# h's operands without the norm's factor, pair products in block 0, and another order of VectorE's work on a pair and on the bank sums

## The chip, the cores and the metric

The kernel runs on one core of one Trainium2 chip. The metric is the device time of one execution in microseconds (us); the kernel before takes 1032.63 us, the median of three runs (1032.61 to 1032.65). Five engines work side by side, each through its own list of instructions in order: TensorE (PE, matmuls and transposes), VectorE (DVE), ScalarE (ACT), GpSimd (POOL) and SyncE (SP, which issues most loads). They wait for each other by semaphores.

## The reference

One layer on 256 rows of 2048 values: a mix of differential attention and a convolution, projected and added to x, and then a SwiGLU block. The change is in the second half:

```python
h = h + jnp.einsum('bsm,md->bsd', mixed, w_out[l])
hn = rms_norm(h, norm2_g[l])
a = jnp.einsum('bsd,df->bsf', hn, w_gate[l])
bu = jnp.einsum('bsd,df->bsf', hn, w_up[l])
h = h + jnp.einsum('bsf,fd->bsd', jax.nn.silu(a) * bu, w_down[l])
```

rms_norm multiplies each row of h by one factor, 1 / sqrt(mean of its squares + eps), and each column by a gain. All is fp32; the hidden width is 5632.

## The kernel before

**Products.** An fp32 matrix is split in a high part (rounded by a cast on ScalarE) and a low part (what is left, a subtraction on VectorE), and each product is three matmuls: high by high, low by high, high by low. The rows are two tiles of 128 (m = 0, 1), the columns are taken in blocks of 512. A *chunk* is two 128-row slices of a weight: a load of 128x1024 (`raw`), a cast to `whi`, a subtraction to `wlo`, and 12 matmuls of 128x512. A *pair* ("s" in the tables) takes two slices of the gate weight and two of the up weight (`wb`, 128x2048) together and makes of them seven products instead of eight: ScalarE casts three of the tiles to high parts (L1052), VectorE makes four sums and differences of them (`wt`, L1049 to L1051), ScalarE casts these (L1055), VectorE makes the low parts `wlb` (L1058) and `wlt` (L1059), and TensorE does 21 matmuls (L1076 to L1078) into several PSUM banks q. The activations' side of a pair is a set of seven sums and differences of h's quarters, the *forms* (`fhi`, `flo`), made once by `make_forms`.

**The stages that matter.** The out-projection computes h in four column blocks n = 0 to 3; n = 3 comes last, in eight chunks. `out_done(n)` adds each block to h (L828), sums squares for the norm, has TensorE transpose the new columns (`ps_h`, L846, two times four transposes a block), scales them by the gain, and splits them in `hhi` and `hlo`. The feed-forward part follows in 11 blocks of 512 hidden columns, in groups of 4, 4 and 3, each group with a pass through w_down. Block 0 is plain: 8 chunks of gate and 8 of up with h's 16 slices; the norm's factor `rstd2` of each row comes in behind, with the silu (`silu_done`, `up_done`). While block 0 runs, `make_forms` spreads the factor over a tile by two transposes (`ps_r`, L988), multiplies the transposed h by it (`hn`, L996), and makes from that the operands of all later blocks: `chi` and `clo` for the slices that go through chunks, and the forms. Blocks from 1 on are 4 pairs and 8 chunks ("g" of gate, "u" of up) in an order written as a string. Behind the last gate chunk or pair, `bank_sums` adds the banks up on VectorE, `products_done` takes the silu, and behind the block `block_done` adds the rest, multiplies, and has the result transposed (`ps_a`).

**What sets the order.** The program is written chunk by chunk: `run_chunks` loads and casts a chunk up to three ahead (near a pair; else two), splits it two ahead, then issues its matmuls. All else (the out-projection's ends, the forms, the sums) are generators; each takes one step when a chunk's matmuls are half issued and one when all are (`resume`), a pair takes four. A `lag(n)` is n such steps. The engines keep to the order so written. Tiles come from pools: `pre` holds what stages before the feed-forward part need and is closed when h's last columns are transposed; only then `ffn` opens over the same memory. Some low parts (`BY_DMA`) are made by an accumulating DMA of GpSimd instead of VectorE.

Of the kernel before, what the change touches and what calls it, by code (L numbers as in the profile page):

```python
# [12 lines left out]
F32 = mybir.dt.float32  # L13
# [5 lines left out]
P = 128  # L19
# [14 lines left out]
LINE = 128  # L34
EPS = 1e-6
# [51 lines left out]
FIRST_ORDER = "gsggsgsuusuu"  # L87
# [42 lines left out]
def tile_block(  # L130
# [13 lines left out]
    prestack = ExitStack()  # L144
    pre = prestack.enter_context(tc.tile_pool(name="pre", bufs=2))
    small = prestack.enter_context(tc.tile_pool(name="small", bufs=4))
# [4 lines left out]
    h = [pre.tile([P, D], F32, tag=f"h{m}", name=f"h{m}", bufs=1) for m in range(NM)]  # L151
# [325 lines left out]
    def square_sum(src, accum, **kw):  # L477
        junk = pre.tile([P, N], F32, tag="junk", name="junk", bufs=1)
        act.activation(junk[:, : src.shape[-1]], src, AF.Square, accum_out=accum, **kw)
# [106 lines left out]
    def conv_back(b):  # L586
# [37 lines left out]
        for b in range(2):  # L624
            for t in range(NB // 2):
# [6 lines left out]
                for j in range(2):  # L632
# [3 lines left out]
                    hi = pre.tile([P, S], F32R, tag="mchi", name=f"mchi{ct}", bufs=NCT)  # L636
                    lo = pre.tile([P, S], F32R, tag="mclo", name=f"mclo{ct}", bufs=NCT)
# [135 lines left out]
    def attend_values(hd):  # L773
# [29 lines left out]
        for e in range(2):  # L803
            mixa[2 * hd + e] = lhs_pair("a", 2 * hd + e) if hd >= 2 else tuple(
                pre.tile([P, S], F32R, tag=t, name=t, bufs=4) for t in ("mahi", "malo"))
            act.activation(mixa[2 * hd + e][0], pt[:, e, :], AF.Copy, scale=col("sg", e))
# [6 lines left out]
    hT = {}  # L813

    hn = []
# [9 lines left out]
    def out_done(n, ps):  # L825
        cs = slice(n * N, (n + 1) * N)
# [13 lines left out]
        for t in range(0, N // P, 2):  # L840
# [6 lines left out]
            if k % HK == 0:  # L847
                hn.append(early.tile([P, HK, S], F32, tag="wb", name="hn"))
            rows = hn[k // HK][:, k % HK : k % HK + 2, :]
            for i in range(2):  # L850
                act.activation(rows[:, i, :], pt[:, i, :], AF.Copy, scale=col("g2", k + i))
# [3 lines left out]
            for i in range(2):  # L855
                hT[k + i] = (hi[:, i, :], lo[:, i, :])
# [3 lines left out]
        else:  # L860
            yield
            yield
            prestack.close()
            ffn["pool"] = ctx.enter_context(tc.tile_pool(name="ffn", bufs=1))
            start(make_forms())


    ffn = {}
    actT = {}
    sil = {}  # L870

    def silu_done(ps):
        yield
        for m in range(NM):
            sil[m] = ffn["pool"].tile([P, N], F32, tag=f"sum{m}", name="sil")
            act.activation(sil[m], ps[m], AF.Silu, scale=rstd2[m])

    def up_done(j, ps):
        fp = ffn["pool"]
        aa = []  # L880
        for m in range(NM):
            a = fp.tile([P, N], F32, tag=f"sum{2 + m}", name="a")
            dve.scalar_tensor_tensor(a, ps[m], rstd2[m], sil[m], ALU.mult, ALU.mult)
            aa.append(a)
        yield from lag(4)
        yield from transposed(j, aa)

    def transposed(j, aa):
        last = j + 1 in FIRSTS and NDS[group_of(j)[0]] < HD
        b = j - group_of(j)[1]  # L890
        for t in range(N // P // 2):
# [9 lines left out]
            if b < 2 and 2 * t < nd:  # L901
                if not b and not t:
                    raw_act[g] = ffn["pool"].tile([P, 2, nd, S], F32, tag="draw", name="raw_act")
# [30 lines left out]
    def make_down_forms(g):  # L934
# [20 lines left out]
        hs = ffn["pool"].tile([P, 2, nd, P], F32R, tag="dhs", name="dhs")  # L955
# [12 lines left out]
        ls = ffn["pool"].tile([P, 4, nd, P], F32R, tag="draw", name="dls")  # L968
# [407 lines left out]
```

## Time and profile before

The profiled execution's own time is its span of 1030.8 us, 1.8 us under the median of the runs, which takes in what lies around the span.

| | |
|---|---|
| median of 3 runs | 1032.63 us |
| span of the profiled execution | 1030.8 us |
| TensorE clock granted | 1.000 |
| DMA, mean over the span | 232 GB/s |
| casts of weights on ScalarE (L326), 256 of them | 264.2 us |
| wlo on VectorE (L335), 208 of them | 250.4 us |
| wlt on VectorE (L1059), 61 of them | 139.8 us, and 19.7 us of waiting for the cast L1055 |

In the profile a row of a timeline is: start, length, engine, line, operation, output<-inputs, sizes and type, how many in a row; in brackets the time for which the engine stood idle before it and what it waited for. The length of a matmul's row is from its entry to its end; since matmuls are pipelined, the distance between starts is what one costs. The same holds for VectorE and ScalarE in a small measure.

### The profile page before, as it was taken

What the parts mean: (1) busy time and instruction counts of PE and PEld (TensorE: products, weight loads), DVE (VectorE), ACT (ScalarE), POOL (GpSimd) and SP (SyncE); (2) the same over time, 40 slices, a digit from 0 to 9 for tenths busy, and PEclk for the clock granted to TensorE, in tenths of its full rate; (3) what the DMA queues carried; (4) which work ended last, traced back from release to release, by engine and by line L of the source; (5) the groups of instructions that cost most, each with busy time, mean ns of one, the idle gap of its engine ahead of it and who ended that gap; (6) DMA issues with size and microseconds to landing.
All of it is one profiled execution on the core that took longest, in us unless ns stands there. A gap on an engine that the chain in (4) does not pass through costs nothing.

```text
span 1030.8 us, 13034 instructions
## 1 busy us (share of the span) xinstructions
PE 1025.7 (100%) x4642; PEld 849.4 (82%) x4642; DVE 929.2 (90%) x1128; ACT 643.4 (62%) x786; POOL 102.7 (10%) x146
## 2 busy tenths in 40 slices
PE   9999999999999999999999999999999999999998
PEld 8888888888888888888888888888888888888887
DVE  6899999999765699999999898989999989889998
ACT  7644656665756675676666556667757556657562
POOL 0300112111000000100102101101001111010020
PEclk9999999999999999999999999999999999999999
DMA  9757555544466677997989799889798979897776
GB/s 338 254 194 258 190 184 164 158 169 166 141 215 214 197 262 222 282 265 210 254 259 272 251 257 270 258 234 262 228 269 255 285 207 283 247 267 218 226 200 174
DMA packets 116448, 238.64 MB, mean 232 GB/s; under 512 B 7840, under 2 KB 9120, under 8 KB 116384
## 3 DMA queue, kind: packets, MB, share of 16 engines
q1 hardware_dynamic: 105216, 203.58, 59.3%
q0 software_dynamic: 10880, 34.08, 17.0%
q8 instruction: 36, 0.59, 0.2%
q14 instruction: 28, 0.23, 0.1%
q10 hardware_dynamic: 288, 0.16, 0.1%
HBM read 204.24 MB, written 9.44 MB: 207 GB/s over the span
## 4 chain that ended last, share of the span: by engine, by line
PE 100%; POOL 0%; DVE 0%; issue 0%; POOLq 0%
PE acc L365 11%; PE acc L366 11%; PE acc L371 11%; PE q L1097 11%; PE q L1103 11%; PE q L1098 11%; PE q L1078 9%; PE q L1077 9%; PE q L1076 9%; PE ps_a L898 1%; PE ps_s L712 1%; PE ps_o L782 1%; PE ps_warm L164 0%; PE ps_h L846 0%; PE ps_qk L693 0%; PE ps_at L802 0%
## 5 line engine op out<-in xcount | busy, mean ns | idle before, releaser
L326 ACT CAST whi<-raw 128x1024 fp32r<-128x1024 f32 (+1 forms) x256 | 264.2, 1043 | 143.8 <-PE acc L366 86.6
L335 DVE TENSOR_TENSOR wlo<-raw,whi 128x1024 fp32r<-128x1024 f32 (+1 forms) x208 | 250.4, 1214 | 38.2 <-ACT whi L326 38.0
L1055 ACT CAST wh<-wt 128x2048 fp32r<-128x2048 f32 x61 | 116.8, 1915 | 109.9 <-DVE wt L1051 109.7
L1059 DVE TENSOR_TENSOR wlt<-wt,wh 128x2048 fp32r<-128x2048 f32 x61 | 139.8, 2291 | 19.8 <-ACT wh L1055 19.7
L1097 PE MATMUL q<-whi,chi 128*128 128x512 f32 x320 | 125.2, 391 | 0.0
L1098 PE MATMUL q<-whi,clo 128*128 128x512 f32 x320 | 124.6, 389 | 0.0
L365 PE MATMUL acc<-whi,xhi 128*128 128x512 f32 x312 | 124.1, 398 | 0.0
L366 PE MATMUL acc<-whi,xlo 128*128 128x512 f32 x312 | 122.2, 392 | 0.0
L1076 PE MATMUL q<-wh,fhi 128*128 128x512 f32 x280 | 109.8, 392 | 0.0
L1077 PE MATMUL q<-wh,flo 128*128 128x512 f32 x280 | 109.0, 389 | 0.0
L1058 DVE TENSOR_TENSOR wlb<-wb,wh 128x1536 fp32r<-128x1536 f32 x61 | 106.8, 1751 | 1.0 <-ACT wh L1052 1.0
L572 DVE SCALAR_TENSOR_TENSOR y<-upad,cw,y 128x256 f32<-128x256 f32 x240 | 101.6, 490 | 0.0
L330 POOL DMA_DIRECT2D wlo<-raw x48 | 41.5, 865 | 555.7 <-ACT wlo L329 286.3
L1052 ACT CAST wh<-wb 128x1536 fp32r<-128x1536 f32 x61 | 89.8, 1472 | 1.0 <-DMA wb<-in_w_down_dram 1.0
L1103 PE MATMUL q<-wlo,chi 128*128 128x512 f32 x320 | 85.7, 390 | 0.0
L371 PE MATMUL acc<-wlo,xhi 128*128 128x512 f32 x312 | 85.2, 394 | 0.0
L1049 DVE TENSOR_TENSOR wt<-wb 128x1024 f32<-128x1024 f32 x61 | 74.4, 1220 | 0.0
L1097 PE MATMUL q<-whi,ahi 128*128 128x512 f32 x182 | 71.0, 390 | 0.0
L1098 PE MATMUL q<-whi,alo 128*128 128x512 f32 x182 | 70.9, 389 | 0.0
L1103 PEld LDWEIGHTS q<-wlo,chi 128*128 128x128 f32 x320 | 60.0, 188 | 12.7 <-DMA wlo<-raw 0.3
L1097 PEld LDWEIGHTS q<-whi,chi 128*128 128x128 f32 x320 | 60.1, 188 | 12.3
L1098 PEld LDWEIGHTS q<-whi,clo 128*128 128x128 f32 x320 | 60.1, 188 | 12.2
(260 smaller groups left out, 1850.5 us busy)
## 6 DMA issues: line engine op xcount, KB each, us to landing
raw<-in_w_in_dram SPq DMA_DIRECT2D x78, 512.0 KB, 4.6
raw<-in_w_gate_dram SPq DMA_DIRECT2D x48, 512.0 KB, 5.0
raw<-in_w_up_dram SPq DMA_DIRECT2D x48, 512.0 KB, 5.3
wlo<-raw POOLq DMA_DIRECT2D x48, 512.0 KB, 7.1
raw<-in_w_down_dram SPq DMA_DIRECT2D x46, 512.0 KB, 6.2
wb<-in_w_down_dram SPq DMA_DIRECT2D x42, 512.0 KB, 5.9
wb<-in_w_up_dram SPq DMA_DIRECT2D x40, 512.0 KB, 4.4
wb<-in_w_gate_dram SPq DMA_DIRECT2D x40, 512.0 KB, 5.5
```

The lines of the kernel that those rows point to most:

```text
L326: act.copy(c["hi"], c["raw"])
L335: dve.tensor_tensor(c["lo"], c["raw"], c["hi"].bitcast(F32), ALU.subtract)
L365: pe.matmul(ps[m], xhi[:, ms], hi[:, j, :], start=c["first"] and j == 0, stop=False)
L366: pe.matmul(ps[m], xlo[:, ms], hi[:, j, :], start=False, stop=False)
L371: pe.matmul(ps[m], xhi[:, ms], lo[:, j, :], start=False, stop=c["last"] and j == nk - 1)
L1055: act.copy(c["hi"][:, :SUMMED], c["t"])
L1059: dve.tensor_tensor(lot, c["t"], c["hi"][:, :SUMMED].bitcast(F32), ALU.subtract)
L1076: pe.matmul(ps, hi, c["hi"][:, w], start=bool(first), stop=False)
L1077: pe.matmul(ps, lo, c["hi"][:, w], start=False, stop=False)
L1097: pe.matmul(ps, xs[i][0][:, ms], hi[:, i, :], start=i == 0 and bool(c["first"].get(qs[m])), stop=False)
L1098: pe.matmul(ps, xs[i][1][:, ms], hi[:, i, :], start=False, stop=False)
L1103: pe.matmul(sum_bank(c, qs[m]), xs[i][0][:, ms], lo[:, i, :], start=False, stop=i == 1 and bool(c["last"].get(qs[m])))
```

## The change

- **Factor.** h's operands carry the gain only. The norm's factor comes in at the silu of each block: `products_done` gives it to the Silu as its scale, and multiplies the silu by it once more with a Copy on ScalarE (so silu(a) times the factor, which makes up for the up half). `rep`, `ps_r`, `rb`, the four multiplications of `hn`, the `hhi`/`hlo` splits of h and the plain block's `silu_done` and `up_done` go.
- **Operands.** `out_done` writes `chi` and `clo` from the transposes in PSUM (n = 1 and 3) or the rows that the forms are made of (n = 0 and 2). The forms are started behind n = 2, so that they are made while n = 3 is multiplied.
- **Block 0** becomes a block of 4 pairs and 8 chunks, in the order "gugsgsgsusuu"; it takes its banks from the two PSUM pools the other way round (`swap`), and none of its low parts by DMA.
- **Pools.** What lives to the end of the out-projection (h, the small tiles, the operands of the mix) moves to `keep` and `small`; `ffn` opens at n = 0, and a pool `late` (wlb, wlt, the sums) opens when h's last columns are transposed, on the memory of `keep`. A pair's first low part therefore waits for the last copies of h to memory.
- **A pair on VectorE.** The four sums, the low parts and now two casts of 1024 are written in turn instead of one kind after the other.
- **Bank sums.** The six additions come in another order.

```diff
-FIRST_ORDER = "gsggsgsuusuu"
+ORDERS = {0: "gugsgsgsusuu", 1: "gsggsgsuusuu"}
...
     def out_done(n, ps):
+        if not n:
+            prestack.close()
+            ffn["pool"] = fp = ctx.enter_context(tc.tile_pool(name="ffn", bufs=1))
...
-            hi, lo = lhs_two("h", k)
-            act.copy(hi, rows)
-            dve.tensor_tensor(lo, rows, hi.bitcast(F32), ALU.subtract)
+            if k % HK < NS:
+                rows = ffn["rows"][:, k // HK, k % HK : k % HK + 2, :]
+                for i in range(2):
+                    act.activation(rows[:, i, :], pt[:, i, :], AF.Copy, scale=col("g2", k + i))
+            else:
+                a = REST.index(k)
+                hi, lo = (ffn[x][:, a : a + 2, :] for x in ("chi", "clo"))
+                for i in range(2):
+                    act.activation(hi[:, i, :], pt[:, i, :], AF.Copy, scale=col("g2", k + i))
+                for i in range(2):
+                    dve.scalar_tensor_tensor(lo[:, i, :], pt[:, i, :], col("g2", k + i), hi[:, i, :].bitcast(F32),
+                                             ALU.mult, ALU.subtract)
...
+        if n == HK * P // N:
+            yield
             start(make_forms())
+        if n == D // N - 1:
+            yield
+            yield
+            keepstack.close()
+            ffn["late"] = ctx.enter_context(tc.tile_pool(name="late", bufs=1, side="right"))
...
     def round_pair(c):
-        assert "pair" in forms
+        while "pair" not in forms or "late" not in ffn:
+            resume()
...
     def split_pair(c):
-        act.copy(c["hi"][:, :SUMMED], c["t"])
-        dve.tensor_tensor(lob, c["b"][:, 1:], c["hi"][:, SUMMED:].bitcast(F32), ALU.subtract)
-        dve.tensor_tensor(lot, c["t"], c["hi"][:, :SUMMED].bitcast(F32), ALU.subtract)
+        act.copy(hi[:, 2:SUMMED], t[:, 2:])
+        rest(lob[:, :1], b[:, 1:2], hi[:, SUMMED : SUMMED + 1])
+        next(sums, None)
+        rest(lob[:, 1:], b[:, 2:], hi[:, SUMMED + 1 :])
+        next(sums, None)
+        act.copy(hi[:, :2], t[:, :2])
+        rest(lot[:, 2:], t[:, 2:], hi[:, 2:SUMMED])
+        rest(lot[:, :2], t[:, :2], hi[:, :2])
...
         dve.tensor_tensor(u2, q[Q6], w1, ALU.add)
+        dve.tensor_tensor(w1, q[Q2], w1, ALU.add)
         dve.tensor_tensor(u3, q[Q7], u2, ALU.add)
+        dve.tensor_tensor(u2, q[Q5], u2, ALU.add)
         dve.tensor_tensor(w4, q[Q5], u3, ALU.add)
-        dve.tensor_tensor(u2, q[Q5], u2, ALU.add)
-        dve.tensor_tensor(w1, q[Q2], w1, ALU.add)
         dve.tensor_tensor(u3, q[Q4], u3, ALU.add)
...
-        for t in g:
-            act.activation(t, t, AF.Silu)
+        for m, t in enumerate(g):
+            act.activation(t, t, AF.Silu, scale=rstd2[m])
+            act.activation(t, t, AF.Copy, scale=rstd2[m])
```

`rest(lo, raw, h)` is the subtraction of a low part; `next(sums, None)` writes the next of the two sums t[1] and t[0], whose lines were L1050 and L1051; t[2:4] (L1049) is now written by `first_sums` from `round_pair`.

The first place is TensorE's list where the out-projection ends and block 0 begins. Before (mchi is the mix's operand, hhi h's, acc the banks; the last out chunk's end, the first gate chunk, the first transposes of h's last columns):

```order
L371 MATMUL acc<-wlo,mchi_2868 128x512
L365 MATMUL acc<-whi,hhi_2958 128x512
L366 MATMUL acc<-whi,hlo_2959 128x512
...
L371 MATMUL acc<-wlo,hhi_2958 128x512 x4
L846 MATMUL ps_h<-ident,h_81 128x128
L846 MATMUL ps_h<-ident,h_82 128x128
L846 MATMUL ps_h<-ident,h_81 128x128
L846 MATMUL ps_h<-ident,h_82 128x128
L365 MATMUL acc<-whi,hhi_2983 128x512
```

And now:

```order
L374 MATMUL acc<-wlo,mchi_2875 128x512
L852 MATMUL ps_h<-ident,h_88 128x128
L852 MATMUL ps_h<-ident,h_89 128x128
L852 MATMUL ps_h<-ident,h_88 128x128
L852 MATMUL ps_h<-ident,h_89 128x128
L852 MATMUL ps_h<-ident,h_88 128x128
L852 MATMUL ps_h<-ident,h_89 128x128
L852 MATMUL ps_h<-ident,h_88 128x128
L852 MATMUL ps_h<-ident,h_89 128x128
L1085 MATMUL q_3371<-whi,chi 128x512
```

All eight transposes of n = 3 now stand directly behind the out-projection's last matmul and ahead of the first gate chunk (since `round_pair` of the first pair, three chunks ahead, takes steps of the generators until `late` is open); before, the first four stood behind that chunk and the other four in the middle of the next.

The second place is VectorE's list at the same point, from the additions of n = 2 to the first pair. Before (the forms then stand in block 0, further down):

```order
L828 TENSOR_TENSOR h_82<-h_82,acc 128x512
L854 TENSOR_TENSOR hlo_3166<-hn,hhi_3165 128x512
L335 TENSOR_TENSOR wlo<-raw,whi 128x1024
L854 TENSOR_TENSOR hlo_3191<-hn,hhi_3190 128x512
L335 TENSOR_TENSOR wlo<-raw,whi 128x1024 x7
L828 TENSOR_TENSOR h_81<-h_81,acc 128x512
L828 TENSOR_TENSOR h_82<-h_82,acc 128x512
```

And now, from the forms' third operation on:

```order
L989 TENSOR_TENSOR sums<-hn 128x512
L990 TENSOR_TENSOR sums<-hn,sums 128x512
L995 TENSOR_TENSOR flo<-hn,fhi 128x512 x2
L338 TENSOR_TENSOR wlo<-raw,whi 128x1024
L997 SCALAR_TENSOR_TENSOR flo<-hn,fhi 128x512
L998 TENSOR_TENSOR flo<-sums,fhi 128x512
L1000 TENSOR_TENSOR flo<-sums,fhi 128x1536
L338 TENSOR_TENSOR wlo<-raw,whi 128x1024 x3
L834 TENSOR_TENSOR h_88<-h_88,acc 128x512
L834 TENSOR_TENSOR h_89<-h_89,acc 128x512
L842 TENSOR_REDUCE ssh<-ss_0_143 128x1
L842 TENSOR_REDUCE ssh<-ss_1_144 128x1
```

The forms moved from block 0 to between the low parts of the out-projection's last chunks; one low part fewer stands ahead of h's additions.

The third place is VectorE's list for a pair. Before, the second pair of block 1:

```order
L1049 TENSOR_TENSOR wt<-wb 128x1024
L1050 TENSOR_TENSOR wt<-wb,wt 128x512
L1051 TENSOR_TENSOR wt<-wt,wb 128x512
L1058 TENSOR_TENSOR wlb<-wb,wh 128x1536
L1059 TENSOR_TENSOR wlt<-wt,wh 128x2048
L335 TENSOR_TENSOR wlo<-raw,whi 128x1024
```

And now, the first pair of block 0:

```order
L1024 TENSOR_TENSOR wt<-wb 128x1024
L338 TENSOR_TENSOR wlo<-raw,whi 128x1024
L1038 TENSOR_TENSOR wlb<-wb,wh 128x512
L1028 TENSOR_TENSOR wt<-wb,wt 128x512
L1038 TENSOR_TENSOR wlb<-wb,wh 128x1024
L1029 TENSOR_TENSOR wt<-wt,wb 128x512
L1038 TENSOR_TENSOR wlt<-wt,wh 128x1024 x2
```

No operation reads what the one directly ahead of it wrote; there are seven for a pair where there were five.

More of the change, by code (lines that the diff above doesn't have):

```diff
@@ L825, in out_done @@
     def out_done(n, ps):
+        if not n:
+            prestack.close()
+            ffn["pool"] = fp = ctx.enter_context(tc.tile_pool(name="ffn", bufs=1))
+            ffn["rows"] = fp.tile([P, 2, NS, S], F32, tag="wh", name="hn", bufs=2)
+            for t in ("chi", "clo"):
+                ffn[t] = fp.tile([P, len(REST), S], F32R, tag=t, name=t)
         cs = slice(n * N, (n + 1) * N)
@@ L859, in out_done @@
             h_squares(n, cs)
-        else:
+        if n == HK * P // N:
+            yield
+            start(make_forms())
+        if n == D // N - 1:
             yield
             yield
-            prestack.close()
-            ffn["pool"] = ctx.enter_context(tc.tile_pool(name="ffn", bufs=1))
-            start(make_forms())
+            keepstack.close()
+            ffn["late"] = ctx.enter_context(tc.tile_pool(name="late", bufs=1, side="right"))
     ffn = {}
+    plain = {}
     actT = {}
[L870 to L886, printed above, removed]
     def transposed(j, aa):
@@ L1131, in multiply_two, with fast_block @@
             start(c["done"](c["sums"]))
-    def fast_block(order, pairs, twos, sources, operands, half, whole, by_dma=dict(g=(), u=())):
+    def fast_block(order, pairs, twos, sources, operands, half, whole, by_dma=dict(g=(), u=()), swap=False):
         units, sums = [], {}
@@ L1138, in fast_block @@
             what = left[kind].pop(0)
-            c = dict(kind=kind, sums=sums, done=None, first={}, last={}, rows=what["rows"], **operands)
+            c = dict(kind=kind, sums=sums, swap=swap, done=None, first={}, last={}, rows=what["rows"], **operands)
             if kind == "s":
@@ L1158, in gate_up_block @@
     def gate_up_block(j):
[L1159 removed]
+        fast_block(ORDERS.get(j, ORDER), [dict(p=p, rows=slice(p, p + HK + 1, HK)) for p in range(NS)],
                    [dict(ks=ks, rows=slice(ks[0], ks[1] + 1, ks[1] - ks[0]), k=ks) for ks in TWOS],
                    dict(g=(w_gate, j * N), u=(w_up, j * N)),
[L1162 removed]
+                   dict(pairs=lambda: forms.get("pair"), plain=plain.get),
                    products_done, lambda sums: block_done(j, sums),
[L1164 removed]
+                   BY_DMA if j > 1 and j not in FIRSTS else dict(g=(), u=BY_DMA["u"] if j else ()), swap=not j)
     def down_pass(g, j0, nb):
@@ L1183, in bank_sums @@
     def bank_sums(q):
-        w1, u2, u3, w4 = (ffn["pool"].tile([P, N], F32, tag=f"sum{i}", name=f"sum{i}") for i in range(4))
+        w1, u2, u3, w4 = (ffn["late"].tile([P, N], F32, tag=f"sum{i}", name=f"sum{i}") for i in range(4))
         act.copy(w1, q[Q1])
@@ L1306, in tile_block @@
         for j in range(j0, j0 + nb):
[L1307 to L1313 removed]
+            gate_up_block(j)
         down_pass(g, j0, nb)
```

102 lines of the change are left out of this document (36 added, 66 removed).

## The prediction

> **What bounds the kernel now.** The page comes first: who is busy, at what clock, and through whom the chain that ended last runs.
>
> ```profile
> PE 1025.7 (100%) x4642; PEld 849.4 (82%) x4642; DVE 929.2 (90%) x1128; ACT 643.4 (62%) x786; POOL 102.7 (10%) x146
> PEclk9999999999999999999999999999999999999999
> PE 100%; POOL 0%; DVE 0%; issue 0%; POOLq 0%
> ```
>
> TensorE is busy for 1025.7 of 1030.8 us, at full clock in every slice, and the whole chain is its own work. So time is won only by fewer matmuls, and lost wherever TensorE is made to wait. VectorE comes next with 90%. The windows show where its slack lies: the out-projection's last columns, block 0, block 1.
>
> ```profile
> 280.00:338.00 58.00, 58.00 (x271) 47.68 (x270) 35.72 (x45) 34.98 (x56) 3.48 (x6) 1.00 0.59 200
> 338.00:383.00 45.00, 45.00 (x205) 37.13 (x204) 37.36 (x40) 29.85 (x40) 1.99 (x4) 1.00 0.69 221
> 383.00:424.00 41.00, 41.00 (x187) 33.95 (x186) 39.19 (x35) 27.27 (x25) 2.79 (x4) 1.00 0.85 259
> ```
>
> After the length, the busy times are PE, weight load, DVE, ACT, POOL. DVE (third) has 7.6 us free in block 0 and only 1.8 us in block 1. The change makes block 0 a block like block 1, behind a place where DVE has much to do. So TensorE's and DVE's timelines there are what counts.
>
> ```profile
> 338.31 0.39 PE L365 MATMUL acc<-whi,hhi 128*128 128x512 f32 x1
> ...
> 341.03 0.67 PE L846 MATMUL ps_h<-ident,h 128*128 128x128 f32 x4
> 341.46 0.48 PE L365 MATMUL acc<-whi,hhi 128*128 128x512 f32 x1
> ...
> 343.40 0.60 PE L846 MATMUL ps_h<-ident,h 128*128 128x128 f32 x4
> 343.75 1.17 PE L371 MATMUL acc<-wlo,hhi 128*128 128x512 f32 x4
> ...
> 350.22 0.38 PE L988 MATMUL ps_r<-ident,rep 128*128 128x128 f32 x2
> ...
> 383.10 0.39 PE L1097 MATMUL q<-whi,chi 128*128 128x512 f32 x1
> ...
> 386.28 0.39 PE L1078 MATMUL q<-wlt,fhi 128*128 128x512 f32 x1
> ```
>
> Block 0 starts at 338.31, block 1 at 383.10; at 386.28 the first pair of block 1 takes its low parts (wlt, the last thing DVE makes for a pair). From 338.31 to 341.03 are 12 matmuls: 0.227 us each, 2.72 a chunk, 4.76 a pair (21). Four transposes take 0.43 and 0.35, so about 0.11 each. Behind 386.28 the two programs issue the same matmuls, and TensorE doesn't wait there now; **when this matmul can start after the change, plus any later new wait, is the answer.**
>
> **The change part by part.** *TensorE alone.* Block 0 falls from 16 chunks (192 matmuls) to 4 pairs and 8 chunks (180): 12 x 0.227 = 2.72 us less; the two ps_r transposes go too (some 0.2). Against it, the eight transposes of h's last columns, now covered by the first gate chunks, stand in front of the first one, and nothing lies ahead of them to multiply while h is added up.
>
> *h's last columns.* VectorE's rows there now:
>
> ```profile
> 335.97 1.23 DVE L335 TENSOR_TENSOR wlo<-raw,whi 128x1024 fp32r<-128x1024 f32 x1 [1.50 <-ACT whi L326]
> 338.69 1.23 DVE L335 TENSOR_TENSOR wlo<-raw,whi 128x1024 fp32r<-128x1024 f32 x1 [1.49 <-ACT whi L326]
> 339.83 1.28 DVE L828 TENSOR_TENSOR h<-h,acc 128x512 f32<-128x512 f32 x2
> ```
>
> It waits 1.5 us before each wlo, which is its slack. The change puts the nine operations of the forms (eight of 512 columns, one of 1536: 6.5 us) and the casts on ScalarE that they take turns with between the wlo of the last chunks. Prices of both, from where they stand today:
>
> ```profile
> 366.66 0.69 DVE L1016 SCALAR_TENSOR_TENSOR sums<-sums,hn 128x512 f32<-128x512 f32 x1
> 367.27 0.68 DVE L1021 TENSOR_TENSOR sums<-hn 128x512 f32<-128x512 f32 x1
> ...
> 373.15 1.75 DVE L1032 TENSOR_TENSOR flo<-sums,fhi 128x1536 fp32r<-128x1536 f32 x1
> 374.82 3.49 DVE L335 TENSOR_TENSOR wlo<-raw,whi 128x1024 fp32r<-128x1024 f32 x3
> ```
>
> ```profile
> 363.26 0.62 ACT L1019 ACTIVATE fhi<-hn 128x512 fp32r<-128x512 f32 x1
> 363.79 1.24 ACT L876 ACTIVATE sil<-acc,rstd 128x512 f32<-128x512 f32 x2
> ...
> 367.99 1.49 ACT L1024 CAST fhi<-sums 128x1536 fp32r<-128x1536 f32 x1 [2.02 <-DVE sums L1021]
> 369.38 0.61 ACT L1025 CAST fhi<-sums 128x512 fp32r<-128x512 f32 x1
> ```
>
> On VectorE starts lie 0.60 apart for 512 columns, 1.67 for 1536, and (3.49 - 1.22) / 2 = 1.135 for 1024; on ScalarE 0.53 for a cast of 512, 1.39 for 1536, and for 1024 between them (some 1.0). The rows of h for n=2 are scaled on ScalarE at about 321 (six chunks before 337.4); behind them stand two squares (0.76 each, rows below), a cast of whi (1.0), three form casts (1.6), whi (1.0), then, with VectorE's wlo and difference between, the casts of four forms (1.9), and only then the whi of the last chunk but one, done at about 331.9. VectorE follows: wlo 1.14, three form operations 0.60 + 0.60 + 1.67, three wlo 3.41. So **h is added from 339.3**, where now it starts at 339.83 behind one wlo more. TensorE's sums would be there at 338.05, so 1.2 us of this is DVE's lateness. The second addition ends at 340.6, and 8 transposes later the first gate chunk starts at 341.5: 3.2 us after 338.31, of which transposes would have cost 0.8 anyway.
>
> *The first pair.* ScalarE goes on with squares and scalings as it does now:
>
> ```profile
> 340.54 0.63 ACT L479 ACTIVATE junk<-h 128x512 f32<-128x512 f32 x1 [1.89 <-DVE h L828]
> ...
> 341.30 0.63 ACT L479 ACTIVATE junk<-h 128x512 f32<-128x512 f32 x1
> ...
> 341.93 0.82 ACT L851 ACTIVATE hn<-ps_h,cols 128x256 f32<-128x256 f32 x2
> ```
>
> That is 2.1 us from h's addition (339.83) to the first scaling (341.93), so 341.4 after the change; four scalings at 0.41 end at 343.1, and the last two of four clo operations follow. Of 256 columns on VectorE the convolution gives the price, 0.49 less the 0.09 by which neighbours overlap above:
>
> ```profile
> L572 DVE SCALAR_TENSOR_TENSOR y<-upad,cw,y 128x256 f32<-128x256 f32 x240 | 101.6, 490 | 0.0
> ```
>
> So the first pair's work on VectorE begins at 343.9. What such a pair costs now, in block 1:
>
> ```profile
> 389.41 1.22 DVE L1049 TENSOR_TENSOR wt<-wb 128x1024 f32<-128x1024 f32 x1
> 390.67 0.69 DVE L1050 TENSOR_TENSOR wt<-wb,wt 128x512 f32<-128x512 f32 x1
> 391.39 0.69 DVE L1051 TENSOR_TENSOR wt<-wt,wb 128x512 f32<-128x512 f32 x1
> 392.00 1.75 DVE L1058 TENSOR_TENSOR wlb<-wb,wh 128x1536 fp32r<-128x1536 f32 x1
> 394.06 2.29 DVE L1059 TENSOR_TENSOR wlt<-wt,wh 128x2048 fp32r<-128x2048 f32 x1 [0.31 <-ACT wh L1055]
> 396.28 1.22 DVE L335 TENSOR_TENSOR wlo<-raw,whi 128x1024 fp32r<-128x1024 f32 x1
> 397.41 1.22 DVE L1049 TENSOR_TENSOR wt<-wb 128x1024 f32<-128x1024 f32 x1
> ```
>
> A pair and its wlo take 8.0 us. The two operations that read their predecessor start 1.26 and 0.72 behind it, not 1.135 and 0.60, and 0.31 goes on a wait for the cast. Interleaved and with the cast in halves this becomes 1.135 (t[2:4]), 0.60, 0.60, 1.135, 0.60, 1.135, some 0.07 for the second half of the cast, 1.135: 6.41, with wlo **7.55, so 0.45 saved a pair**. TensorE needs 4.76 + 2.72 = 7.48 for the same. With the second gate chunk's wlo in between, the first pair's wlt is ready at 343.9 + 7.55 = 351.5. TensorE, three chunks behind 341.5, wants it at 341.5 + 8.16 + 0.45 = 350.1 and **waits 1.4 us**. The weights' loads are no part of this; the first low part also waits until h's copies to memory have landed:
>
> ```profile
> DMA to landing us min/median/max: 3.9/4.8/5.2
> ```
>
> Issued at 340.7, they land by 345.9, just ahead of the first wlb at 346.2; I count 0, at most 1 us.
>
> *From there to block 1* VectorE doesn't stop: three more pairs (19.23), six wlo (6.81; the change takes none of block 0's by DMA), t[2:4] of block 1's first pair (1.14), the bank sums and the rest of that pair (5.28). The sums now:
>
> ```profile
> 461.93 0.69 DVE L1189 TENSOR_TENSOR sum<-q,sum 128x512 f32<-128x512 f32 x1
> 462.72 0.69 DVE L1190 TENSOR_TENSOR sum<-q,sum 128x512 f32<-128x512 f32 x1
> 463.33 0.68 DVE L1191 TENSOR_TENSOR sum<-q,sum 128x512 f32<-128x512 f32 x1
> ```
>
> A sum that reads its predecessor starts 0.80 behind it, another 0.60. In the new order none reads its predecessor's result, but the second, fourth and sixth overwrite a tile that the predecessor still reads, and wait for it all the same: three waits instead of two, 4.2 us instead of 4.0. Together 19.23 + 6.81 + 1.14 + 4.2 + 5.28 = 36.7: wlt for block 1's first pair at **388.15**. TensorE alone would come to it at 351.5 + 35.4 = 386.9, and waits again. Against 386.28 that is **+1.87 us**.
>
> *Block 1.* ScalarE now has Silu and a Copy for each half, behind that pair's last cast (388.05). At 0.62 and 0.53 each, from the rows above with their overlap of 0.1, they end at 390.2; the second product of VectorE ends at 391.0. TensorE reaches block 0's first transposes, ten matmuls behind 388.15, at 390.4: **+0.5**. From the second pair on VectorE has its 0.45 a pair, and no wait is left; the later blocks have the same matmuls and two small ScalarE operations more, under ScalarE's 62%.
>
> *Sum:* 1.87 + 0.5 = 2.4 on the profiled execution's 1030.8; the median of the runs lies 1.8 above that span, an offset that I take as it is. 1032.63 + 2.4 = **1035.0 us**.
>
> **A rule against it.** The Trainium skill ("VectorE: DVE Perf Modes", section "The DRAIN you can't avoid") says that after each DVE operation the next doesn't start until the pipeline is empty, that a semaphore between them costs nothing, and that one should minimize the count of operations. By it the interleaving gains nothing and the added pieces cost. The rows speak against it: 461.93 + 0.69 lies before 462.72, where the next one reads it, but 462.72 + 0.69 behind 463.33: an operation that waits for nothing starts before its predecessor ends.
>
> **The rivals.** *The interleaving brings nothing* (by this mechanism the 1.26 and 0.72 stay whatever stands between): 1.26 + 0.72 + 0.72 + 0.60 + 3 x 1.135 = 6.7 a pair, 0.3 more on five pairs, 1.5 us: 1036.5. Against it the 0.60 above. Chance 0.08.
> *VectorE isn't late at h* (not slower): if ScalarE comes to the casts of the forms earlier than reckoned, and h is added at 338.1, all behind it comes 1.2 earlier: 1033.8. It decides from the cast of the last whi but one: done before 330.7 it holds. Chance 0.22.
> *VectorE catches up in block 0* (not slower): 7.55 against 7.48 is within 1%; if it runs ahead of TensorE after the first pair, 386.9 - 386.28 + 0.5 = +1.1, 1033.7; without the wait for the first pair either, -0.8, 1031.8. Chance 0.15.
> *Both*, and nothing waits: -2.0 (2.95 of matmuls and ps_r removed, 0.9 of transposes uncovered): 1030.6. Chance 0.07.
> *The bank sums don't do what they say*: as reckoned, 0.2 a block, beside TensorE's work.
>
> **How the numbers follow.** The forecast has 0.48. A measurement tells about 0.2%, 2.07 us, from no change: 1030.56 to 1034.70. The forecast's own spread is some 0.8 us to both sides, of which a quarter lies below 1034.70. Slower: 0.36 + 0.08 = 0.44; same: 0.12 + 0.22 + 0.12 = 0.46; faster: 0.07 and 0.03 of the catching up, since with 2.95 us of work removed the best case only just gets there. The range takes in the rivals but the best, and above them the interleaving's price and the landing: 1031.0 to 1036.8.
>
> **What would show it.** In the changed profile the first addition of h's last columns starts at 339 or later (right) or 338.1 (wrong); TensorE's first gate matmul of block 0 at about 341.5; the first L1066 at 351.5, some 1.4 us behind its L1065; DVE without idle time from 344 to 388 at 7.5 us a pair; bank sums 0.60 and 0.80 apart in turn; the first ps_a a little late. Wrong it is if DVE shows waits for ScalarE in block 0 (then it is worse), or if TensorE has no gap behind the first gate chunk.

## The result, and the profile after

| | before | changed |
|---|---|---|
| median of the runs | 1032.62 us (4 runs, 1032.48 to 1032.65) | 1043.65 us (4 runs, 1042.71 to 1044.83) |
| ratio, 95% interval | | 1.0108 (1.0094 to 1.0122) |
| span of the profiled execution | 1030.8 us | 1043.1 us |

The kernel became slower by 11.0 us; 2.4 were predicted, and the time lies above the range. The profiled execution is the longest of the four (1044.83). The page of the changed kernel, busy times, granted clock by slices, and the chain's shares by engine:

```profile
PE 1029.5 (99%) x4628; PEld 849.1 (81%) x4628; DVE 942.2 (90%) x1272; ACT 667.1 (64%) x861; POOL 102.3 (10%) x146
PEclk9999999999999999999999999999999999999998
PE 86%; DVE 5%; issue 5%; DMA 3%; ACT 1%; POOL 0%; DVEq 0%; POOLq 0%; ACTq 0%
```

The chain was TensorE alone; now 14% of it runs through others, and the last slice is below full clock. TensorE's waits (whole time, how many, the longest) name the places:

```profile
PE q L1091 <- DMA wlo<-raw: 4.5, 3, 3.9
PE ps_h L852 <- DVE h L834: 1.7, 2, 1.5
PE q L1066 <- DVE wlt L1038: 0.7, 2, 0.5
PE q L1066 <- issue: 0.6, 1, 0.6
PE ps_a L893 <- DVE sum L1203: 0.5, 1, 0.5
```

The last four are the waits of blocks 0 and 1 that were predicted. The first wasn't. It helps to match each matmul of the changed kernel with the same one of before, and to follow how much later it starts: 2.4 us at 386.28 (before's time), 3.2 at 388.66, 3.3 at 405, 4.8 at 999, 9.0 at 1005.5, and 11.9 from 1008.6 to the end. So 3.2 us are lost around blocks 0 and 1, some 1.5 trickle in over 600 us (0.6 of it two short waits of the first kind), and **7.1 us are lost in one place, some 30 us before the end**. There, in TensorE's timeline:

```profile
1010.16 0.39 PE L1086 MATMUL q<-whi,alo 128*128 128x512 f32 x1
1014.45 2.07 PE L1091 MATMUL q<-wlo,ahi 128*128 128x512 f32 x4 [3.90 <-DMA wlo<-raw]
```

and in the windows (length, then busy time and count of PE, weight load, DVE, ACT, POOL, then clock, DMA share, GB/s), first at block 0's start, then here:

```profile
338.00:342.00 4.00, 2.26 (x12) 1.60 (x11) 2.70 (x6) 2.70 (x8) 1.41 (x4) 0.91 0.93 301
342.00:346.00 4.00, 4.00 (x13) 3.11 (x12) 3.92 (x6) 3.17 (x5) 0.57 (x1) 0.66 0.82 291
...
1014.00:1018.00 4.00, 3.55 (x8) 2.81 (x9) 4.00 (x5) 2.09 (x3) 0.00 (x0) 0.50 1.11 249
1018.00:1022.00 4.00, 4.00 (x14) 3.16 (x13) 3.53 (x4) 1.90 (x3) 0.76 (x2) 0.68 0.54 97
```

After the gap the granted clock is 0.50, matmuls start 0.43 us apart instead of 0.227, and that lasts some 6 us: 4.2 us of waiting cost 2.9 more. At block 0's start the clock fell too (0.66 from 342 to 346); there TensorE came to the first low part at 351.5 instead of the 350.1 that were predicted, and would have waited for it anyway. That it cost nothing is luck: the prediction had no such fall, and in one of the kernels below it comes later and costs time. Who made the DMA late is read backwards on the engines that feed it. VectorE and ScalarE of the changed kernel in the last pass through w_down:

```profile
991.43 1.22 DVE L1024 TENSOR_TENSOR wt<-wb 128x1024 f32<-128x1024 f32 x1
994.67 0.69 DVE L1176 TENSOR_TENSOR sum<-q,sum 128x512 f32<-128x512 f32 x1 [2.02 <-ACT sum L1174]
...
998.11 0.69 DVE L1181 TENSOR_TENSOR sum<-q,sum 128x512 f32<-128x512 f32 x1
...
1001.05 0.69 DVE L1029 TENSOR_TENSOR wt<-wt,wb 128x512 f32<-128x512 f32 x1
```

```profile
994.05 0.59 ACT L1174 COPY sum<-q 128x512 f32<-128x512 f32 x1 [0.88 <-PE q L1066]
...
1001.77 1.05 ACT L1045 CAST wh<-wt 128x1024 fp32r<-128x1024 f32 x1 [6.19 <-DVE wt L1029]
1002.73 1.05 ACT L329 CAST whi<-raw 128x1024 fp32r<-128x1024 f32 x1
1003.68 1.05 ACT L332 ACTIVATE wlo<-raw 128x1024 fp32r<-128x1024 f32 x1
```

```profile
1005.09 0.88 POOL L333 DMA_DIRECT2D wlo<-raw  x1 [11.94 <-ACT wlo L332]
```

And the same place before:

```profile
989.39 0.69 DVE L1051 TENSOR_TENSOR wt<-wt,wb 128x512 f32<-128x512 f32 x1
990.18 0.69 DVE L1188 TENSOR_TENSOR sum<-q,sum 128x512 f32<-128x512 f32 x1
...
990.11 1.92 ACT L1055 CAST wh<-wt 128x2048 fp32r<-128x2048 f32 x1
...
993.74 1.05 ACT L329 ACTIVATE wlo<-raw 128x1024 fp32r<-128x1024 f32 x1
...
995.15 0.88 POOL L330 DMA_DIRECT2D wlo<-raw  x1 [6.49 <-ACT wlo L329]
```

Before, all of a pair's sums t stood ahead of the bank sums, and ScalarE cast them while VectorE added banks. Now only t[2:4] does (L1024, 991.43); t[1] and t[0] stand between the low parts, and VectorE's list holds the bank sums ahead of them. The first of these waits 2.02 us for ScalarE's copy of a bank (L1174), which waits for TensorE. t[0] is written at 1001.05. ScalarE stands 6.19 us before its second half cast, and behind that cast, in the same list, are the cast and the scaling from which an accumulating DMA makes a chunk's low part. The DMA is issued 9.9 us later, 5.1 more than TensorE's own lateness of 4.8, and then takes 9.3 us to land, where that of before took 7.7.

### The profile page after: what moved, and what is told of

It reads as the page before. It is cut to its first block, busy times and chain, and to the rows that moved or that the text cites. A ratio compares the mean times of both kernels' runs of the same rounds, so it can differ in the third digit from the quotient of the medians.

```text
span 1043.1 us, 13192 instructions
## 1 busy us (share of the span) xinstructions
PE 1029.5 (99%) x4628; PEld 849.1 (81%) x4628; DVE 942.2 (90%) x1272; ACT 667.1 (64%) x861; POOL 102.3 (10%) x146
## 4 chain that ended last, share of the span: by engine, by line
PE 86%; DVE 5%; issue 5%; DMA 3%; ACT 1%; POOL 0%; DVEq 0%; POOLq 0%; ACTq 0%
PE q L1091 10%; PE acc L368 10%; PE acc L369 10%; PE acc L374 10%; PE q L1085 9%; PE q L1086 9%; PE q L1066 8%; PE q L1065 8%; PE q L1064 8%; DMA wlo<-raw 3%; DVE wlo L338 1%; PE ps_a L893 1%; DVE wlb L1038 1%; PE ps_s L715 1%; PE ps_o L785 0%
## 5 line engine op out<-in xcount | busy, mean ns | idle before, releaser
L329 ACT CAST whi<-raw 128x1024 fp32r<-128x1024 f32 (+1 forms) x248 | 254.7, 1042 | 104.3 <-PE acc L369 76.3
L338 DVE TENSOR_TENSOR wlo<-raw,whi 128x1024 fp32r<-128x1024 f32 (+1 forms) x200 | 239.7, 1209 | 39.6 <-ACT whi L329 39.4
L1038 DVE TENSOR_TENSOR wlt<-wt,wh 128x1024 fp32r<-128x1024 f32 x130 | 157.8, 1222 | 0.0
L1045 ACT CAST wh<-wt 128x1024 fp32r<-128x1024 f32 x65 | 68.5, 1055 | 129.3 <-DVE wt L1029 129.1
L1038 DVE TENSOR_TENSOR wlb<-wb,wh 128x512 fp32r<-128x512 f32 (+1 forms) x130 | 123.9, 953 | 17.6 <-ACT wh L1017 16.6
L1085 PE MATMUL q<-whi,chi 128*128 128x512 f32 x352 | 138.7, 394 | 0.0
L1086 PE MATMUL q<-whi,clo 128*128 128x512 f32 x352 | 137.9, 392 | 0.0
L1064 PE MATMUL q<-wh,fhi 128*128 128x512 f32 x308 | 120.8, 392 | 0.0
L1065 PE MATMUL q<-wh,flo 128*128 128x512 f32 x308 | 120.0, 390 | 0.0
L1091 PE MATMUL q<-wlo,chi 128*128 128x512 f32 x352 | 94.4, 390 | 0.6 <-DMA wlo<-raw 0.6
L1040 ACT CAST wh<-wt 128x1024 fp32r<-128x1024 f32 x65 | 68.3, 1051 | 39.5 <-DVE wt L1024 39.5
L1024 DVE TENSOR_TENSOR wt<-wb 128x1024 f32<-128x1024 f32 x65 | 79.2, 1218 | 0.0
L1085 PEld LDWEIGHTS q<-whi,chi 128*128 128x128 f32 x352 | 66.5, 189 | 13.8
```

The source lines that it names most:

```text
L329: act.copy(c["hi"], c["raw"])
L338: dve.tensor_tensor(c["lo"], c["raw"], c["hi"].bitcast(F32), ALU.subtract)
L1038: dve.tensor_tensor(lo, raw, h.bitcast(F32), ALU.subtract)
L1064: pe.matmul(ps, hi, c["hi"][:, w], start=bool(first), stop=False)
L1065: pe.matmul(ps, lo, c["hi"][:, w], start=False, stop=False)
L1085: pe.matmul(ps, xs[i][0][:, ms], hi[:, i, :], start=i == 0 and bool(c["first"].get(qs[m])), stop=False)
```

## The experiments

Times are medians; the kernel before ran beside each, at 1032.40 to 1032.72. "Late by" is the difference of matched matmuls, as above.

**The last pass's sums ahead again.** The first pair behind the last block writes t[1] and t[0] at once, all else as changed.

```diff
     first_sums(c, dve)
+    if c is eager[0]:
+        for _ in last_sums(c, dve):
+            pass
+        c["summed"] = True
```

> The changed kernel, with one pair's work written otherwise: for the first pair of the last pass through w_down the sums t[1] and t[0] stand where they stood in the kernel before, ahead of the bank sums. Theory (the late loss is an order effect: t[0] moved behind the bank sums, ScalarE's second half cast waits 6.2 us for it, and behind that cast stands the scaling that GpSimd's accumulating DMA of wlo needs): the DMA is issued some 5 us earlier against TensorE, the 3.9 us wait at 1010 and the half clock behind it (2.9 us) go, about 1036.5 us (-7.1). Rival (the DMA lands late by itself, 9.3 us against 7.7 before, from traffic of the same moment): at most 2 us better, over 1041. Rival (the clock drop is a thing of its own): the wait goes, the drop stays, about 1039.5.

Measured: 1040.54 us, ratio 1.0074 (1.0062 to 1.0086). The DMA is issued at 999.10 instead of 1005.09, and its wait of 3.9 us is gone. But a second wait stood behind the first: the load of a later pair's weight is late. The cast that takes it starts 14.4 us after the load was issued (counted here and below from the first of its two halves) and has waited 4.8 us for it. ScalarE's timeline, and the window in which TensorE waits for what follows from it:

```profile
1014.42 1.48 ACT L1017 CAST wh<-wb 128x1536 fp32r<-128x1536 f32 x1 [4.84 <-DMA wb<-in_w_down_dram]
```

```profile
1018.00:1022.00 4.00, 1.86 (x4) 1.05 (x5) 4.00 (x5) 3.00 (x4) 0.46 (x1) 0.76 0.85 194
```

TensorE stands 2.5 us and falls to half clock again; late by 8.2 at the end instead of 11.9. The cause of the first wait is shown, the number was wrong by the second.

**The pair as before, in the changed kernel.** Four sums, one cast of 2048, two low parts, in the old order everywhere.

```diff
-        act.copy(hi[:, 2:SUMMED], t[:, 2:])
-        rest(lob[:, :1], b[:, 1:2], hi[:, SUMMED : SUMMED + 1])
-        next(sums, None)
...
+        act.copy(hi[:, :SUMMED], t)
+        dve.tensor_tensor(lob, b[:, 1:], hi[:, SUMMED:].bitcast(F32), ALU.subtract)
+        dve.tensor_tensor(lot, t, hi[:, :SUMMED].bitcast(F32), ALU.subtract)
```

> The changed kernel with a pair's work on VectorE and ScalarE in the order of the kernel before (three sums first, one cast of 2048, wlb whole, wlt whole); block 0, factor and bank sums as changed. Theory of the late loss: it goes here too (-7.1). In block 0 a pair and its wlo take 8.0 us on VectorE instead of 7.55, five pairs, so block 1's first pair comes 2.2 us later: about 1038.8. Rival (interleaving gains nothing on VectorE): about 1036.5.

Measured: 1039.88 us, 1.0069 (1.0057 to 1.0081): faster than the changed kernel. TensorE's waits for wlt rise to 2.9 us in five, and it is late by 4.2 at 405, against 3.3: the interleaving is worth 0.9 us over blocks 0 and 1 (0.8 at block 1's first low parts, where 2.2 were expected). At the end the DMA is in time, and the same load of a weight late (13.1 us from issue), with a gap of 2.0 us that doesn't bring the clock down:

```profile
1018.00:1022.00 4.00, 2.41 (x11) 1.57 (x10) 3.79 (x3) 3.12 (x4) 0.53 (x1) 1.00 0.91 231
```

**The new pair alone, in the kernel before.** The converse edit: block 0, operands and bank sums as before, only the pair in the new order.

> The kernel before with only the pair's work on VectorE and ScalarE in the new order; block 0 plain, bank sums old. Theory of the late loss: the same wait and half clock appear, since they hang on this order alone: 1032.6 + 4 to 7 = 1037 to 1040. Rival (the lateness of 4.8 us that the changed kernel brings along is needed for it): within 1 us of before.

Measured: 1040.59 us, 1.0070 (1.0056 to 1.0083).

```profile
PE q L1111 <- DMA wlo<-raw: 3.9, 1, 3.9
```

TensorE is on time within 0.5 us until 999, then waits 4.2 us and loses 3.0 at half clock. So the pair's order by itself makes the whole late loss, and no part of block 0's.

**The same with the last pass's sums ahead, and then with transfers held back.** In the second, GpSimd reads a word of the last wlt before it issues the additions of h's halves in memory (hd), so that these come at 1009 instead of directly behind the low part's DMA, and so after the load that was late. The same edit issues the loads of h's last columns (`hend`, in `fetch_end`) five steps later.

```diff
-            yield from lag(HD_LAG)
+            yield from lag(HD_LAG if FGROUPS[g] > 3 else 8)
+            if FGROUPS[g] == 3:
+                hold = const.tile([P, 1], F32, tag="hold", name="hold")
+                pool.tensor_scalar(hold, lots[-1][:, 0, :1].bitcast(F32), 1.0, 0.0, ALU.mult, ALU.add)
...
-            if FGROUPS[g] > 3:
-                yield from lag(HD_LAG)
+            yield from lag(HD_LAG if FGROUPS[g] > 3 else 5)
             for m in range(NM):
                 pool.dma_start(out=hd[m][:, (n + 1) * N : (n + 2) * N], in_=us[m], accum_op=ALU.add)
         if g == len(FGROUPS) - 1 and not at_end(g, n):
             fetch_end()
```

> The kernel before with the new pair order (third experiment) but t[1] and t[0] of the last pass's first pair ahead of the bank sums. Theory: the wait for wlo's DMA at 1005 goes; without block 0's change the end is that of the kernel before: 1032.4, within 0.5 us. Rival (the interleaving slows the end in other ways, as the rest that stayed in the first two experiments): 1034 to 1037.

> The seventh experiment's kernel (kernel before, new pair order, t[1] and t[0] of the last pass's first pair ahead of the bank sums), with one small GpSimd operation ahead of the four accumulating DMAs of the pass before the last, which reads the low part of a later pair: so they are issued some 8 to 10 us later (the edit of the fifth experiment had left their issue where it was). Theory (wb's load is late there, 13.5 us against 9.9 before, because these transfers run beside it): wb lands within 10 us, TensorE doesn't wait at 1014, the end is the kernel before's: 1032.4, within 0.6. Rival (another cause): as there, 1037.4.

Measured: 1037.40 us, 1.0043 (1.0031 to 1.0056), and 1034.65 us, 1.0022 (1.0012 to 1.0032). In the first the cast takes the weight 13.5 us after the issue of its load, in the second 9.4 us, and ScalarE doesn't wait for it; in the kernel before it is 9.9. ScalarE's timelines of the two:

```profile
1010.23 1.49 ACT L1048 CAST wh<-wb 128x1536 fp32r<-128x1536 f32 x1 [3.98 <-DMA wb<-in_w_down_dram]
```

```profile
1007.91 1.49 ACT L1048 CAST wh<-wb 128x1536 fp32r<-128x1536 f32 x1
```

What moved from 1003 to 1007 (packets, MB, share of the DMA engines' time; q0 is GpSimd's queue, q1 that of the loads), in the first and then in the second, where q0 moves nothing:

```profile
q0 software_dynamic: 254, 0.47, 68.0%
q1 hardware_dynamic: 226, 0.46, 42.0%
```

```profile
q1 hardware_dynamic: 587, 1.14, 101.4%
```

The loads move 0.46 MB beside the additions and 1.14 MB without them. The edit moved `hend` too, from directly behind the late load to behind another weight's (at 1000.87), but that alone doesn't mend it: in the three kernels with more lag steps, further down, `hend` has this place while the additions have the old one, and there the weight still takes 13.8 to 14.2 us. So the second wait is one of transfers that meet: GpSimd's additions in memory beside the load. In the first kernel's profiled execution, one of its shorter ones (1035.88), it costs 2.3 us; in the second nothing is lost there. What is left of the time is a wait of 1.7 us for a low part's DMA at 963, where the first has 0.5; its cause wasn't sought. Even without its harm at the end, the new order of a pair doesn't beat the old in the kernel before, which has no wait for it to save.

**Both mends in the changed kernel.** Sums of the last pass ahead, hd held back. Once with a new tile of one number per partition, as in the diff above, once with the number written into a tile that exists:

```diff
-                hold = const.tile([P, 1], F32, tag="hold", name="hold")
-                pool.tensor_scalar(hold, lots[-1][:, 0, :1].bitcast(F32), 1.0, 0.0, ALU.mult, ALU.add)
+                pool.tensor_scalar(eps1s[:, :1], lots[-1][:, 0, :1].bitcast(F32), 1.0, 0.0, ALU.mult, ALU.add)
```

> The changed kernel with both edits of the last pass (sums ahead, accumulating DMAs held). Theory: nothing is left at the end but the lateness from block 0 (3.3 to 4.0 us in all traces with the changed block 0): 1036.1, within 0.8. Rival (lateness from block 0 upsets the end by itself): 1038 or more.

> The tenth experiment's kernel, but the small GpSimd operation writes to a column that is there already instead of to a new tile of 4 bytes a partition. Theory (in the tenth the waits of the last pass were gone, but every matmul from 280 us on took 0.2295 instead of 0.2269 us, because the new tile moved the operands' tiles): matmuls at 0.2269 again, no wait after 400 us, only the lateness from block 0 (3.3 to 4.5 us) is left: 1036.5, within 1. Rival (the held transfers slow the matmuls): 1043 as there.

Measured: 1044.03 us, 1.0116 (1.0101 to 1.0132), with the new tile, though TensorE waits nowhere after 392; 1037.66 us, 1.0049 (1.0035 to 1.0063), without, 0.2 above the range that was expected. In the second only the waits of blocks 0 and 1 are left (beside one at the kernel's start that all have):

```profile
PE ps_h L852 <- DVE h L834: 1.7, 2, 1.5
...
PE q L1071 <- DVE wlt L1042: 0.5, 1, 0.5
PE ps_a L893 <- DVE sum L1209: 0.5, 1, 0.5
PE q L1071 <- issue: 0.3, 1, 0.3
```

TensorE is late by 2.9 at 388.66, 3.1 at 405 and 3.3 at the end. This is what the prediction spoke of, without the late loss. Its profiled execution is the shortest of its five runs (1036.27 to 1038.29), so what the longer ones lose isn't seen.

**The tile alone.** The changed kernel with a tile of four bytes per partition that nothing uses.

```diff
+    const.tile([P, 1], F32, tag="hold", name="hold")
```

> The changed kernel with a tile of 4 bytes a partition more among the constants, which nothing uses. Theory (placement of the operands): matmuls from 280 us on take 0.2295 instead of 0.2269 us, some 7 us more: 1050. Rival (placement is nothing): 1043.65.

Measured: 1052.24 us, 1.0195 (1.0179 to 1.0211), 8.6 us over the changed kernel (5.9 between the two profiled executions). From 400 to 800 us matmuls start 0.2295 us apart instead of 0.2270. By groups (count, busy time, mean length in ns) between 400 and 600, the changed kernel and then this one:

```profile
L1066 PE MATMUL q<-wlt,fhi 128*128 128x512 f32 x48 | 18.7, 390 | 0.0
```

```profile
L1067 PE MATMUL q<-wlt,fhi 128*128 128x512 f32 x47 | 18.7, 397 | 0.0
```

The pairs' matmuls that read `fhi` are 7 ns longer with `wlt` and 5 with `wh` (392 to 397), those that read `flo` 2, the chunks' hardly (389 to 390 for `whi` by `ahi`). The kernel before with the new pair and the held transfers has the same new tile, and there they start 0.2270 apart. That the tile makes it is shown; by which address isn't.

**Tries at block 0's loss.** First, h's last transposes behind a gate chunk again: the pair's own wait for `late` moves from the casts to the low parts.

```diff
-        while "pair" not in forms or "late" not in ffn:
+        while "pair" not in forms:
             resume()
...
+        while "late" not in ffn:
+            resume()
```

> The changed kernel with the wait for the pool late moved from the rounding of a pair to its splitting, one chunk later, so that the first gate chunk stands ahead of the transposes of h's last columns again. Theory (block 0 is lost at both ends, by the uncovered transposes and by VectorE's chain from h to block 1): TensorE's 1.86 us gap behind the last out chunk and the half clock behind it go, but block 1's first pair is set by VectorE, which can start the first pair some 1 us earlier only: 1 to 1.5 us better, the late loss stays: about 1042.4. Rival (the gap itself is the loss): 3 us better, 1040.6.

Measured: 1047.07 us, 1.0142 (1.0129 to 1.0155), slower still. h is now added at 341.8, behind a pair's first sums and one more low part, so its copies to memory start and land later, and VectorE waits 2.4 us for them. TensorE stands 3.7 us, at half clock behind it, and is late by 5.6 at 383 instead of 1.7. The cover for 0.9 us of transposes was paid with h's lateness.

Then the same with h in a pool of its own, so that the wait for its copies should go, with low parts by DMA too; and, without the cover, block 0's low parts of up by DMA (2.3 us less on VectorE). All three put the last pass's sums ahead and try to move the additions in memory by more lag steps; the third does nothing else. Each is built on the one shown behind it, which its expectation calls the kernel above.

> The kernel above with u by DMA, and three edits at the start of block 0: h's last columns are added at once behind the last out chunk, the wait for the pool late stands at the splitting of a pair (so the first gate chunk lies around h's transposes), and h has a pool of its own so that the first low parts lie on the operands of the mix and wait for no copy of h to memory. Theory: the wait for h's copies (0.74 us here, 2.36 us in the fourth experiment) is what made the fourth experiment slower, and h's late addition behind two more operations; without both the first pair's wlt is ready at about 349 instead of 352.2, TensorE waits 1.4 us there and nowhere else, and block 1's first pair comes some 2 us earlier than in the kernel before: 1031. Rival (the copies don't matter): as e6, 1035, or slower as the fourth experiment was.

> The kernel above, with block 0's second and fourth up chunk split by the accumulating DMA as in block 1 (two wlo of 1.14 us less on VectorE in block 0). Theory (block 0 is bound by VectorE's chain from h's addition to block 1's first pair): that pair's wlt comes 2.3 us earlier, TensorE's own time binds from 1.3 us on, so the lateness at block 1's first pair falls from 2.4 to about 1.1 us: 1035.1. Rival (the loss is all at the start of block 0, VectorE keeps up behind it): no difference, 1036.4.

> The first experiment's kernel (t[1] and t[0] of the last pass's first pair ahead of the bank sums) with the four accumulating DMAs of the pass before it, and the loads of h's last columns behind them, three steps later. Theory (what was left at the end there, a wait of 2.1 us and half clock behind it, is the load of wb that shares the DMA engines with those transfers: they began 1 us earlier beside it than in the kernel before): wb lands within 9 us, TensorE doesn't wait at 1000 to 1025, and what is left is the loss of 3.3 to 4 us around block 0: 1036.4. Rival (wb is late for another reason): as the first experiment, 1040.5.

Measured: 1042.82 us (1.0102, 1.0088 to 1.0115), 1041.95 (1.0094, 1.0079 to 1.0110) and 1041.78 (1.0092, 1.0078 to 1.0105). In the first the wait for h's copies is still 1.4 us, though h has its own pool (why isn't shown), and TensorE stands 4.1. In the second the low parts by DMA bring 0.2 of the 2.3 us taken from VectorE (late by 3.0 to 3.1 behind block 1's first pair, against 3.2 to 3.3): VectorE stands 0.8 and 1.4 us for ScalarE's casts instead. More lag steps left the additions where they were, 0.55 us behind the low part's DMA, and moved only `hend`; the weight's load stayed late, so moving `hend` alone doesn't mend it, and the held additions above took the place of this test. The third also shows what block 0 can cost: its block 0 is the changed kernel's, but the clock falls at 353 instead of 341, behind TensorE's wait for the first pair, and it is late by 4.6 at 388.66 instead of 3.2.

Last, the sums t of the first five pairs on GpSimd (with the held transfers and the new tile, so at the longer matmuls):

> The kernel above with the three sums (t[2:4], t[1], t[0]) of the first five pairs, block 0's four and block 1's first, on GpSimd instead of VectorE. Theory (block 0's loss is VectorE's chain): VectorE has 2.3 us a pair less to do, the first pair's wlt is ready at about 350.7, then TensorE alone binds, and block 1's first pair is within 0.5 us of the kernel before: 1033. Rival (GpSimd is slow, 0.8 us for 64 columns in the kernel before, and takes VectorE's time): above 1036.

Measured: 1050.36 us, 1.0171 (1.0157 to 1.0185). In GpSimd's timeline:

```profile
353.05 3.32 POOL L1032 TENSOR_TENSOR wt<-wb 128x1024 f32<-128x1024 f32 x1 [3.43 <-DVE wlt L1046]
```

It takes 3.3 us for an addition of 128x1024 that VectorE makes in 1.2, and waits 3.4 for its buffers before. VectorE's own operations become longer beside it. The first low parts from 344 to 388 (count, busy time, mean length in ns), here and then in the same kernel with the sums on VectorE:

```profile
L1046 DVE TENSOR_TENSOR wlb<-wb,wh 128x512 fp32r<-128x512 f32 x4 | 9.4, 2362 | 0.8 <-DMA hd<-h 0.8
```

```profile
L1042 DVE TENSOR_TENSOR wlb<-wb,wh 128x512 fp32r<-128x512 f32 x5 | 3.4, 685 | 0.9 <-DMA hd<-h 0.9
```

So both halves of the rival hold: GpSimd is slow and takes VectorE's time. TensorE is late by 10.5 at 386. None of these kernels beats the one before.

## Why the prediction was wrong

**The early part held, step by step.** In the changed kernel's timelines of VectorE and TensorE:

```profile
339.11 1.28 DVE L834 TENSOR_TENSOR h<-h,acc 128x512 f32<-128x512 f32 x2
...
343.64 1.22 DVE L1024 TENSOR_TENSOR wt<-wb 128x1024 f32<-128x1024 f32 x1
...
346.73 0.69 DVE L1038 TENSOR_TENSOR wlb<-wb,wh 128x512 fp32r<-128x512 f32 x1 [0.74 <-DMA hd<-h]
...
353.16 1.22 DVE L1024 TENSOR_TENSOR wt<-wb 128x1024 f32<-128x1024 f32 x1
...
360.72 1.22 DVE L1024 TENSOR_TENSOR wt<-wb 128x1024 f32<-128x1024 f32 x1
```

```profile
341.18 0.68 PE L1085 MATMUL q<-whi,chi 128*128 128x512 f32 x1
...
352.32 0.47 PE L1066 MATMUL q<-wlt,fhi 128*128 128x512 f32 x1 [0.62 <-issue]
...
388.70 0.50 PE L1066 MATMUL q<-wlt,fhi 128*128 128x512 f32 x1 [0.53 <-DVE wlt L1038]
...
391.86 0.55 PE L893 MATMUL ps_a<-ident,sum 128*128 128x128 f32 x3 [0.46 <-DVE sum L1203]
```

- h added: 339.3 predicted, 339.11 measured. First gate matmul 341.5, 341.18. First pair's work on VectorE 343.9, 343.64.
- First wlt: 351.5, measured 352.32. The step that was mis-sized is "I count 0, at most 1 us" for the copies of h: 0.74. They took 5.9 us to land, where the slowest before took 5.2.
- A pair and a wlo: 7.55, and 360.72 - 353.16 = 7.56. The rule that was weighed against it doesn't hold here: neighbours start 0.60 apart. The section of the Trainium skill that it was taken from ("VectorE: DVE Perf Modes", "The DRAIN you can't avoid") itself says that a next operation which isn't held starts earlier; the prediction left that out.
- Block 1's first wlt: 388.15, measured 388.70; its ps_a 0.5 late, measured 0.5. Together 3.2 us late instead of 2.4; the landing's 0.74 us is the largest part of the difference.
- Bank sums: 4.2 predicted, 4.0 before. They take 383.28 - 379.24 = 4.04 in block 0: no gain, and not the loss of 0.2 that was reckoned.

```profile
379.24 0.68 DVE L1176 TENSOR_TENSOR sum<-q,sum 128x512 f32<-128x512 f32 x1
380.02 0.69 DVE L1177 TENSOR_TENSOR sum<-q,sum 128x512 f32<-128x512 f32 x1
380.63 0.68 DVE L1178 TENSOR_TENSOR sum<-q,sum 128x512 f32<-128x512 f32 x1
381.35 0.69 DVE L1179 TENSOR_TENSOR sum<-q,sum 128x512 f32<-128x512 f32 x1
...
383.28 0.68 DVE L1038 TENSOR_TENSOR wlb<-wb,wh 128x512 fp32r<-128x512 f32 x1
```

The second and fourth start 0.78 and 0.72 behind their predecessor, the third 0.61: one that overwrites what its predecessor reads waits as one that reads its result does.

**The step that failed** is "From the second pair on VectorE has its 0.45 a pair, and no wait is left; the later blocks have the same matmuls and two small ScalarE operations more". It was argued from TensorE's list and from shares of busy time. It missed that the interleaving moves t[1] and t[0] *behind* the bank sums wherever a pair follows a block's end, and with them the second half cast, and with it all that stands behind that cast on ScalarE. In the blocks TensorE has at most its two short waits from it (0.6 us; whether they have this cause wasn't sought); in the last pass, where a low part by DMA stands right behind and the bank sums first wait 2.02 us, it costs 4.2 us and 2.9 at half clock. The new pair alone in the kernel before shows it (late by 7.2 at the end), and the sums put ahead take that wait away in both kernels. The prediction had this order before it: its sum for block 1's first pair has the bank sums between t[2:4] and the rest of the pair. It followed VectorE there, and not ScalarE and the DMA that wait for t[0] in the last pass.

**What stays open.** Behind the mended wait the load of a weight comes late where GpSimd's additions meet it, and holding them back mends that (two kernels); why it is just in time in the kernel before wasn't tested. The queues' rows only fit: from 999 to 1003 the loads move 0.85 MB there, beside 0.08 MB of GpSimd's, against 0.52 beside 0.24 in the kernel before with the new pair and the last pass's sums ahead. Of block 0's loss the transposes, h's lateness and the copies are seen in the rows, but no kernel here took it away. The trickle of 1.5 us from 405 to 999 shrinks to 0.3 in the kernel with both mends, and its cause wasn't sought beyond the two short waits.

## What to carry to other kernels

When operations are interleaved so that they hide each other's latency, look at every place where something else stands between the first and the last of them: a value that another engine needs must not fall behind work that waits. Follow the consumer's list one step further, to what is queued behind its wait. And expect a wait that is taken away to uncover the next: here two marginal transfers stood one behind the other.

## What the runs showed of the hardware

- **Short gaps can bring the clock down, and their length alone doesn't decide.** Single gaps between matmul starts of 2.5, 3.7, 4.1 and 4.3 to 4.7 us brought it to half (matmuls 0.43 us apart); single ones of 2.0 (pair as before) and 2.1 (held transfers) didn't. Of two gaps close together, 2.0 and 0.9 us did (more lag steps, at 1019), and 1.8 and 1.1 didn't (both mends with the new tile, at 350). The gaps of 1.9 and 0.6 at block 0's start, with transposes between, did in the changed kernel and didn't in the one with more lag steps alone. The new pair alone had a granted clock of 1.000 in two of its six runs and took 1036.8 and 1037.3 us there, against 1040.1 to 1041.3 at 0.997 or 0.998. A stage at half clock lasted 3.4 or 6.8 us each time and cost some 1.3 to 3 us. The Trainium skill ("TensorE: Matmul & The Clock Gate", section "Part 1: The HAM clock gate") gives half rate for an idle window of about 3.4 us; here a gap of 2.5 us, 2.1 of it idle, sufficed, so the rule is too mild as a bound.
- **Four bytes cost 8.6 us.** An unused tile among the constants lengthened the pairs' matmuls by `wlt` from 390 to 397 ns in the changed kernel; the same tile, used, cost nothing in the kernel before with the new pair. Whoever adds a small tile for an experiment should look at the matmuls' spacing before reading the time.
